# Scan operands of two directions loaded by one transfer to 128 partitions

## The chip, the cores and the metric

The kernel runs on one core of a Trainium2 chip. The metric is device microseconds of one execution. Five engines work side by side on queues of their own: TensorE (PE for matmuls, PEld for its weight loads), VectorE (DVE), ScalarE (ACT), GpSimd (POOL) and SyncE (SP). Nearly all transfers between DRAM and the on-chip memory of 128 partitions are issued by SP, in the order in which they stand in its queue, and are carried by 16 DMA engines.

## The reference

One layer of a bidirectional encoder on 2048 tokens of width 1024. Three head groups read the same normalised input: neighbourhood attention (6 heads), an mLSTM (4 heads) and a gated delta rule (6 heads). The last two are recurrences over 32 chunks of 64 tokens, once forwards and once backwards; their outputs are added. An output projection, a cross-attention and a feed-forward layer follow.

```python
def step(state, xs):                       # delta rule, one chunk of 64 tokens
    u_c, w_c, a_c, qd_c, ks_c, gl_c = xs
    v_new = u_c - jnp.einsum('bhld,bhde->bhle', w_c, state)
    o = jnp.einsum('bhld,bhde->bhle', qd_c, state) + jnp.einsum('bhls,bhse->bhle', a_c, v_new)
    state = state * jnp.exp(gl_c)[..., None, None] + jnp.einsum('bhld,bhle->bhde', ks_c, v_new)
    return state, o
...
h_fwd = mlstm_direction(qh, kh, vh, ig[0], fg[0])
h_bwd = jnp.flip(mlstm_direction(jnp.flip(qh, 2), ...), 2)
hs = head_rms((h_fwd + h_bwd).transpose(0, 2, 1, 3)).reshape(b, s, ML_WIDTH)
```

In the mLSTM every product is weighted by exponentials of running gate sums, with a running maximum as stabiliser.

## The kernel before

All is in 32 bits. Each product of a weight with an activation is made of three matmuls of rounded parts (`mm3`, L108). The program has three passes and a tail.

- **Pass A** projects the input for the delta rule and the mLSTM and prepares the scans. `gates` makes the gate quantities of a block of 512 tokens and stores the cumulated gates as rows, `g_row` (L405). `gram` does so for a pair of chunks (t of 0 to 15): it loads `kq` and the gate rows `gr` (L420), makes the Gram matrices, and stores for each direction d a tile `sc` of three operands, [token, operand, head, 64], in one store to `sc_d` (L473). The third operand, the keys times decay, is what the scan loads as `kb`. `inv` inverts the triangular matrices into `w_d`. `ml_in` projects q, k, v of the mLSTM and stores q and k to `mlc_d`, laid out [column tile of 128, partition, 2048 tokens] (L547).
- **Pass B** is the two scans, 16 steps of a pair of chunks each. Step m works on pair m forwards and pair 15 - m backwards at once: the forward chunk's rows stand on partitions 0 to 63 and its state's rows on 64 to 127, the backward ones mirrored. `gdn_scan` (delta rule) and `ml_scan` (mLSTM) each have a `load(m)` that fetches the operands of a step while the step before runs, into tiles of one or two buffers: `kb`, `ge`, `qe`, `me`, `mge`, `mqe` and `mkq` have one, so the next load into them waits until they have been read. Since the two directions need different pairs, and different halves of the partitions, each operand is loaded by two transfers of 64 partitions. Between the steps stand projections for the attention (`rest`), so that PE has work while the scans wait.
- **Pass C** is the neighbourhood attention. Its values are loaded by `nav` (L926) from `nav_d`, where rows are tokens of a 32 x 64 grid: a transfer takes up to 4 grid rows of 24 or 32 columns and 384 elements of each, and lays the tokens one on each partition.
- **The tail** is output projection, cross-attention and feed-forward layer.

A scheduler orders each engine's instructions when the program is built. The program then waits on semaphores alone.

Names in the rows below: `ge` is the gates broadcast over 64 partitions for the delta rule (768 elements each), `me` and `mge` are the stabilisers and gate factors of the mLSTM, broadcast likewise (512 elements), `kb` is the keys above, `mkq` and `mqe` are q and k of the mLSTM in two layouts. `gr` in pass A is the same gate rows, for `gram`.

Three of the loads, of the delta rule and the mLSTM, read so:

```python
nc.sync.dma_start(out=kb[CH[d]], in_=self.sc_d[d, t, :, :, 2].rearrange("c s h l -> s c h l"))
nc.sync.dma_start(out=ge[SR[d]], in_=self.g_row[t, :, d][None].broadcast_to([64, 2, 6, 64]))
nc.sync.dma_start(out=kq[:, d], in_=self.mlc_d[:, :, P * t:P * t + P].rearrange("c p l -> p c l"))
```

Of the kernel before, what the change touches and what calls it, by code (L numbers as in the profile page):

```python
# [8 lines left out]
F32 = mybir.dt.float32  # L9
# [4 lines left out]
PSUM = bass.MemoryType.PSUM  # L14
DRAM = bass.MemoryType.DRAM

P = 128
# [32 lines left out]
class Trunk:  # L50
# [26 lines left out]
    def rsqrt(self, out, in_, n):  # L77
        """out = in_ ** -0.5 on GpSimd, [P, n]."""
        self.nc.gpsimd.tensor_tensor(out=out, in0=in_, in1=self.nhalf[:in_.shape[0]].broadcast_to([in_.shape[0], n]), op=ALU.pow)

    def rms_stats(self, sq_sum, n, pspool, small, rs=None, name="psm"):
        """sq_sum [P, n] (partial sums over D per partition) -> PSUM [P, n] with 1/rms of each column on every partition.
        rs: where 1/rms stays, tokens on partitions."""
# [18 lines left out]
    def mm3(self, out, sh, sl, mh, ml, nk):  # L102
        """out += stationary.T @ moving over nk k-tiles, exact to fp32: hi*hi + hi*lo + lo*hi."""
# [8 lines left out]
    def mix(self, late):  # L112
        """x -> y_d, the three head groups' outputs, transposed; late keeps what the last blocks of attention need."""
# [6 lines left out]
        self.mlc_d = dt("mlc_d", [4, P, T])  # L120
# [4 lines left out]
        self.sc_d = dt("sc_d", [2, 16, 2, 64, 3, 6, 64])  # L125
# [27 lines left out]
    def pass_a(self, rest):  # L153
        """Projections of the delta rule and the mLSTM; Gram matrices and inverses of the delta rule."""
        with ExitStack() as st:
# [16 lines left out]
            for b in range(4):  # L172
# [16 lines left out]
                # of the last group first what the first steps of the scan need  # L189
# [7 lines left out]
    def step(self, gen, n, late=0):  # L197
        """n steps of a generator; late: how far behind their place in the program they may run."""
# [4 lines left out]
    def pass_b(self, rest):  # L203
        """The scans, with keys and values of the neighbourhood attention between their steps."""
# [15 lines left out]
    def pass_c(self, late):  # L220
        """Neighbourhood attention, with the last projections and the other heads' outputs between its blocks."""
# [17 lines left out]
    def norm_in(self, b, first=True):  # L239
        """Block b of the input, normalised: self.acts[b % 2]; the first time also the norms."""  # L240
# [3 lines left out]
        # nothing else runs before block 0: its two halves go side by side, in small pieces  # L244
# [37 lines left out]
    def gdn_in(self, b, ct):  # L282
        """q, k, v of the delta rule for one block of tokens, tile ct: projection, convolution, 2 silu, to DRAM.
        The convolution runs two tokens behind the projection."""
# [40 lines left out]
    def zero_w(self):  # L325
        """The blocks of w_d that stay zero."""
# [1073 lines left out]
```

## Time and profile before

| | |
|---|---|
| median of 3 runs | 3787.74 us (3775.37 to 3800.31) |
| span of the profiled execution | 3789.0 us (its record has no other time of its own) |
| PE busy | 3468.7 us, 92% |
| DVE, POOL, ACT busy | 1819.1, 1601.0, 1153.2 us |
| DMA | 466.07 MB in 396663 packets, mean 123 GB/s |
| steps of the scans | first matmul L672 at 856.4 us, last at 1280.2 us |

The page cuts the span into 40 slices of some 95 us. The tenth to the fourteenth hold the scans. A busy share of the DMA engines is a mean over all 16: 0.25 can be four engines that work all the time and twelve that do nothing.

### The profile page before, as it was taken

The numbers are of one execution on the slowest core, as the hardware profiler recorded it, in microseconds if no ns is written. First come the engines' busy times: TensorE is split into PE (matmuls) and PEld (weight loads), VectorE is DVE, ScalarE is ACT, GpSimd is POOL, SyncE is SP. The second block draws the span as 40 slices with busy tenths as digits, with TensorE's granted clock in tenths as the row PEclk, the third lists the DMA queues.
The fourth block names the chain that finished last, engine by engine and source line by source line (L and its number), as shares of the span: only waits on it lengthen the run. The fifth ranks groups of instructions, "written<-read, shape, count | busy, mean of one in ns | idle before, by whom it ended". The sixth has DMA issues, their size and how long they took to land.

```text
span 3789.0 us, 54073 instructions
## 1 busy us (share of the span) xinstructions
PE 3468.7 (92%) x21392; PEld 2774.0 (73%) x21392; DVE 1819.1 (48%) x3257; ACT 1153.2 (30%) x2015; POOL 1601.0 (42%) x947
## 2 busy tenths in 40 slices
PE   5878688888788889999999999999999999999998
PEld 4656566666666655588888887888888778888887
DVE  7697977625666644553443436222222352222224
ACT  3233232232323333544343344222222332222223
POOL 4455444554454531253535445333333453333333
PEclk9988888988899996999999999999999999999999
DMA  4546475678999565742233233111111141111112
GB/s 140 179 132 183 140 193 142 174 181 200 202 215 217 173 216 172 210 174 98 95 134 134 87 123 133 53 45 48 45 50 48 60 138 48 49 53 48 53 47 89
DMA packets 396663, 466.07 MB, mean 123 GB/s; under 512 B 151978, under 2 KB 296826, under 8 KB 393338
## 3 DMA queue, kind: packets, MB, share of 16 engines
q1 hardware_dynamic: 392794, 450.55, 41.2%
q0 software_dynamic: 3616, 12.06, 0.9%
q8 instruction: 169, 2.77, 0.3%
q14 instruction: 84, 0.69, 0.1%
HBM read 360.01 MB, written 102.50 MB: 122 GB/s over the span
## 4 chain that ended last, share of the span: by engine, by line
PE 52%; DVE 1%; ACT 1%; issue 1%; DMA 0%; POOL 0%; POOLq 0%; DVEq 0%; SPq 0%; ACTq 0%
PE psg L108 31%; PE psa L108 21%; PE psa L1180 0%; DVE nh L1005 0%; DVE ss L1016 0%; PE psm L88 0%; PE psm L99 0%; ACT whi L987 0%; DMA out_y<-nh 0%; DMA xb<-x_d 0%; POOL wlo L989 0%; DVE xb L1251 0%; ACT acta L1137 0%; ACT acta L1006 0%; ACT sqt L1015 0%
## 5 line engine op out<-in xcount | busy, mean ns | idle before, releaser
L989 POOL TENSOR_TENSOR wlo<-wraw,whi 128x1024 fp32r<-128x1024 f32 (+2 forms) x401 | 842.0, 2101 | 1294.1 <-ACT whi L987 1271.7
L108 PE MATMUL psg<-acta,whi 128*128 128x512 f32 x3008 | 975.3, 404 | 36.9 <-ACT pad L295 23.2
L108 PE MATMUL psg<-actb,whi 128*128 128x512 f32 (+2 forms) x2752 | 857.4, 393 | 36.8 <-DVE rt L613 10.2
L987 ACT CAST whi<-wraw 128x1024 fp32r<-128x1024 f32 (+2 forms) x417 | 373.5, 896 | 1192.3 <-PE psa L108 551.7
L108 PEld LDWEIGHTS psg<-acta,whi 128*128 128x128 f32 x3008 | 576.7, 194 | 169.2 <-ACT pad L295 25.2
L108 PE MATMUL psa<-ht,whi 128*128 128x512 f32 x2048 | 638.6, 395 | 0.6 <-ACT whi L987 0.5
L108 PEld LDWEIGHTS psg<-actb,whi 128*128 128x128 f32 (+1 forms) x2752 | 518.9, 193 | 148.2 <-ACT pad L295 11.2
L108 PE MATMUL psg<-acta,wlo 128*128 128x512 f32 x1504 | 602.5, 402 | 3.6 <-POOL wlo L989 3.6
L108 PE MATMUL psg<-actb,wlo 128*128 128x512 f32 (+2 forms) x1376 | 539.9, 393 | 27.9 <-POOL wlo L989 27.9
L108 PEld LDWEIGHTS psa<-ht,whi 128*128 128x128 f32 x2048 | 384.0, 188 | 95.1 <-ACT whi L987 1.5
L1229 DVE TENSOR_TENSOR fr<-fr 128x512 f32<-128x512 f32 x128 | 167.9, 1312 | 495.4 <-ACT fr L1228 495.4
L1242 DVE TENSOR_TENSOR xb<-psa,xb 128x512 f32<-128x512 f32 x256 | 175.6, 691 | 476.4 <-PE psa L108 476.3
L108 PE MATMUL psa<-ht,wlo 128*128 128x512 f32 x1024 | 401.0, 396 | 0.7 <-POOL wlo L989 0.7
L108 PEld LDWEIGHTS psg<-acta,wlo 128*128 128x128 f32 x1504 | 290.8, 193 | 67.6 <-POOL wlo L989 5.0
L108 PEld LDWEIGHTS psg<-actb,wlo 128*128 128x128 f32 (+1 forms) x1376 | 265.2, 193 | 86.5 <-POOL wlo L989 33.4
L1232 POOL TENSOR_TENSOR ht<-fr,ht 128x512 fp32r<-128x512 f32 x128 | 169.1, 1321 | 249.1 <-ACT ht L1231 247.8
L108 PEld LDWEIGHTS psa<-ht,wlo 128*128 128x128 f32 x1024 | 192.3, 188 | 47.5 <-POOL wlo L989 1.8
L1016 DVE TENSOR_TENSOR ss<-ss,sqt 128x512 f32<-128x512 f32 (+1 forms) x91 | 123.4, 1356 | 47.0 <-ACT sqt L1015 44.3
L308 DVE SCALAR_TENSOR_TENSOR acc<-pad,vecs,acc 128x512 f32<-128x512 f32 (+2 forms) x144 | 143.6, 1000 | 1.5 <-DVE sm L436 0.6
L1231 ACT CAST ht<-fr 128x512 fp32r<-128x512 f32 x128 | 79.4, 621 | 180.1 <-DVE fr L1229 180.0
L1228 ACT ACTIVATE fr<-psg 128x512 f32<-128x512 f32 x128 | 75.9, 593 | 132.3 <-PE psg L108 132.3
L495 DVE TENSOR_TENSOR tv<-x 72x30 f32<-72x30 f32 (+36 forms) x210 | 94.4, 470 | 2.0 <-DVE x L496 0.6
(376 smaller groups left out, 3982.3 us busy)
## 6 DMA issues: line engine op xcount, KB each, us to landing
wraw<-in_w_ff SPq DMA_DIRECT2D x72, 512.0 KB
wraw<-in_w_ff SPq DMA_DIRECT2D x144, 256.0 KB
wraw<-in_w_gd SPq DMA_DIRECT2D x36, 512.0 KB
sc_d<-sc SPq DMA_DIRECT2D x32, 576.0 KB
xt<-in_xT SPq DMA_DIRECT2D x16, 1024.0 KB
wraw<-in_w_out SPq DMA_DIRECT2D x32, 512.0 KB
wraw<-in_w_xq SPq DMA_DIRECT2D x32, 512.0 KB
wraw<-in_w_xo SPq DMA_DIRECT2D x32, 512.0 KB
```

Source lines behind the costliest of these rows:

```text
L108: nc.tensor.matmul(out=out, lhsT=a(k), rhs=b(k), start=(i == 0), stop=(i == n - 1))
L308: V.scalar_tensor_tensor(out=acc[:, :n], in0=pad[:, p0 + j:p0 + j + n], scalar=cw(j), in1=acc[:, :n], op0=ALU.mult, op1=ALU.add)
L495: V.tensor_tensor(out=tv, in0=m[:, j + 1:32, j:j + 1].broadcast_to([2 * N, n, j]), in1=m[:, j:j + 1, 0:j].broadcast_to([2 * N, n, j]), op= ...
L987: nc.scalar.copy(out=hi, in_=raw)
L989: (lo_eng or nc.gpsimd).tensor_tensor(out=lo, in0=raw, in1=hi.bitcast(F32), op=ALU.subtract)
L1016: nc.vector.tensor_tensor(out=ss, in0=ss, in1=sq, op=ALU.add)
L1228: S.activation(out=r, in_=ps, func=AF.Relu)
L1229: V.tensor_tensor(out=r, in0=r, in1=r, op=ALU.mult)
L1231: S.copy(out=ht[:, 0], in_=r)
L1232: G.tensor_tensor(out=ht[:, 1], in0=r, in1=ht[:, 0].bitcast(F32), op=ALU.subtract)
L1242: V.tensor_tensor(out=xs[nb][:, j], in0=ps, in1=xs[nb][:, j], op=ALU.add)
```

## The change

Three of the delta rule's and mLSTM's operands for both directions get a layout in DRAM in which pair m of the forward direction and pair 15 - m of the backward one are two rows at a fixed distance, so that one transfer can name both, and one transfer fills all 128 partitions: `kb` from a new array `kb_d`, `ge` from a new array `g_st` (in addition to `g_row`, which `gram` still reads), `me` from `mx_row` and `mge` from `ai_row`, which change their order of dimensions or of directions. The source of such a transfer is written as two rows, then 64 (tokens for `kb`, a repetition for the other three), then 768 or 512 elements. In pass A the store of `sc` becomes three: operands 0 and 1, and the halves of `kb`. `g_st` takes 16 small stores for each block of 512 tokens. `mlc_d` is laid out by pair, [pair, partition, column tile, 128], so `mkq` reads 2 KB runs in place of 512 bytes, the store of q and k writes 512-byte runs in place of 2 KB, and `mqe` takes two transfers per direction in place of one. `mx_row` and `ai_row` are stored by two transfers each. Nothing that is computed changes.

```diff
-        self.mlc_d = dt("mlc_d", [4, P, T])
+        self.mlc_d = dt("mlc_d", [16, P, 4, P])
...
-        self.sc_d = dt("sc_d", [2, 16, 2, 64, 3, 6, 64])
+        self.sc_d = dt("sc_d", [2, 16, 2, 64, 2, 6, 64])
+        self.kb_d = dt("kb_d", [2, 16, 64, 2, 6, 64])
+        self.g_st = dt("g_st", [2, 16, 2, 6, 64])
...
         for c in range(2):
             nc.sync.dma_start(out=self.g_row[t4, c].rearrange("t d h l -> t (d h) l"), in_=row[:, 64 * c:64 * c + 64])
 
+            for t in range(4):
+                for d in range(2):
+                    nc.sync.dma_start(out=self.g_st[1 - d, 4 * b + t, c], in_=row[12 * t + 6 * d:12 * t + 6 * d + 6, 64 * c:64 * c + 64])
...
-            nc.sync.dma_start(out=self.sc_d[d, t].rearrange("c s a h l -> (c s) (a h l)"), in_=sc.rearrange("p a h l -> p (a h l)"))
+            nc.sync.dma_start(out=self.sc_d[d, t].rearrange("c s a h l -> (c s) (a h l)"), in_=sc[:, 0:2].rearrange("p a h l -> p (a h l)"))
+            for c2 in range(2):
+                nc.sync.dma_start(out=self.kb_d[d, t, :, c2], in_=sc[64 * c2:64 * c2 + 64, 2])
...
-                nc.sync.dma_start(out=self.mlc_d[ct, :, sl], in_=t)
+                nc.sync.dma_start(out=self.mlc_d[sl.start // P:sl.stop // P, :, ct].rearrange("j p l -> p j l"), in_=t.rearrange("p (j l) -> p j l", l=P))
...
+            nc.sync.dma_start(out=kb.rearrange("p c h l -> p (c h l)"), in_=self.kb_d.rearrange("d t s c h l -> (d t) s (c h l)")[m:32 - m:31 - 2 * m])
             for d in range(2):
...
-                nc.sync.dma_start(out=kb[CH[d]], in_=self.sc_d[d, t, :, :, 2].rearrange("c s h l -> s c h l"))
...
-                nc.sync.dma_start(out=ge[SR[d]], in_=self.g_row[t, :, d][None].broadcast_to([64, 2, 6, 64]))
+            nc.sync.dma_start(out=ge.rearrange("p c h l -> p (c h l)"), in_=self.g_st.rearrange("d t c h l -> (d t) (c h l)")[15 - m:17 + m:2 * m + 1, None].broadcast_to([2, 64, 768]))
...
-                nc.sync.dma_start(out=kq[:, d], in_=self.mlc_d[:, :, P * t:P * t + P].rearrange("c p l -> p c l"))
-                nc.sync.dma_start(out=e[CH[d]], in_=self.mx_row[None, :, d, t].broadcast_to([64, 2, 4, 64]))
+                nc.sync.dma_start(out=kq[:, d], in_=self.mlc_d[t])
...
-                nc.sync.dma_start(out=qe[SR[d]], in_=self.mlc_d[0:2, :, P * t:P * t + P].rearrange("c (h e) l -> e (c h) l", h=2))
-                nc.sync.dma_start(out=ge[SR[d]], in_=self.ai_row[d, t].rearrange("h c l -> (h c l)")[None].broadcast_to([64, 512]).rearrange("p (h l) -> p h l", l=P))
+                for a in range(2):
+                    nc.sync.dma_start(out=qe[SR[d], a::2], in_=self.mlc_d[t, CH[a], 0:2])
+            nc.sync.dma_start(out=e.rearrange("p c h l -> p (c h l)"), in_=self.mx_row.rearrange("d t c h l -> (d t) (c h l)")[m:32 - m:31 - 2 * m, None].broadcast_to([2, 64, 512]))
+            nc.sync.dma_start(out=ge.rearrange("p h l -> p (h l)"), in_=self.ai_row.rearrange("d t h c l -> (d t) (h c l)")[15 - m:17 + m:2 * m + 1, None].broadcast_to([2, 64, 512]))
```

The scheduler orders the changed program anew. In a middle step of the scans SP's queue held these loads before (the last numbers are the destination's partitions and elements):

```order
L637 DMA kb<-sc_d 64x2x384
L640 DMA qe<-gd_c 64x6x128
L641 DMA ge<-g_row 64x2x384
L637 DMA kb<-sc_d 64x2x384
L640 DMA qe<-gd_c 64x6x128
L641 DMA ge<-g_row 64x2x384
L833 DMA mkq<-mlc_d 128x4x128
L836 DMA mqe<-mlc_d 64x4x128
L834 DMA me<-mx_row 64x2x256
L837 DMA mge<-ai_row 64x512
```

In a middle step of the changed program SP's queue holds these:

```order
L641 DMA kb<-kb_d 128x1x768
L847 DMA mqe<-mlc_d 64x2x128
L844 DMA mkq<-mlc_d 128x512 x2
L847 DMA mqe<-mlc_d 64x2x128
L848 DMA me<-mx_row 128x1x512
L648 DMA qe<-gd_c 64x6x128 x2
L649 DMA ge<-g_st 128x1x768
L849 DMA mge<-ai_row 128x1x512
```

The joined loads stand one behind the other in the queue, each once per step, and their destinations are written as 128 x 1 x N, which is how the program spells a transfer whose source has one dimension more, here two rows of 64.

The same spelling stands in pass C of the program before, at the loads of the values, whose sources are 4 (or 3) grid rows of 32 tokens; SP's queue there:

```order
L926 DMA nav<-nav_d 72x1x384
L929 DMA naqb<-nac_d 128x3x128
L920 DMA nab<-in_nab 128x2x352
L926 DMA nav<-nav_d 128x1x384 x2
L926 DMA nav<-nav_d 96x1x384
L929 DMA naqb<-nac_d 128x3x128
```

These loads are the same in both programs; nothing moves here.

In pass A, behind the first block's gates, SP's queue held before:

```order
L417 DMA kq<-gd_c 128x9x128 x2
L405 DMA g_row<-row 4x12x64 x2
L547 DMA mlc_d<-rt 128x512
L420 DMA gr<-g_row 64x768 x4
L985 DMA wraw<-in_w_ml 128x1024
```

SP's queue at the same place in the changed program:

```order
L423 DMA kq<-gd_c 128x9x128 x2
L407 DMA g_row<-row 4x12x64
L411 DMA g_st<-row 6x64 x4
L426 DMA gr<-g_row 64x768
L411 DMA g_st<-row 6x64 x4
L407 DMA g_row<-row 4x12x64
L411 DMA g_st<-row 6x64 x2
L426 DMA gr<-g_row 64x768
L411 DMA g_st<-row 6x64 x6
L426 DMA gr<-g_row 64x768 x2
```

The 16 small stores stand before and among the loads of `gr`, on which the first `gram` of the block depends.

## Rows read from the trace of the kernel before

**Rows 1.** The page: span, engines, 40 slices, and the chain by engine.
```profile
span 3789.0 us, 54073 instructions
...
PE 3468.7 (92%) x21392; PEld 2774.0 (73%) x21392; DVE 1819.1 (48%) x3257; ACT 1153.2 (30%) x2015; POOL 1601.0 (42%) x947
...
PE   5878688888788889999999999999999999999998
...
DMA  4546475678999565742233233111111141111112
...
PE 52%; DVE 1%; ACT 1%; issue 1%; DMA 0%; POOL 0%; POOLq 0%; DVEq 0%; SPq 0%; ACTq 0%
```

**Rows 2.** Five stretches: each engine's busy us, granted clock, DMA share, GB/s.
```profile
core 0: us, PE busy (x) PEld busy (x) DVE busy (x) ACT busy (x) POOL busy (x), PEclk, DMA share, GB/s
812.00:1285.00 473.00, 385.22 (x5493) 315.67 (x5491) 278.63 (x533) 139.06 (x266) 232.64 (x158) 0.91 0.87 203
...
1080.00:1200.00 120.00, 103.09 (x1514) 84.17 (x1509) 77.18 (x149) 37.70 (x73) 59.16 (x43) 0.97 0.96 227
1509.00:1511.00 2.00, 2.00 (x15) 1.67 (x15) 1.41 (x5) 1.56 (x5) 0.00 (x0) 0.50 0.25 86
1513.00:1516.00 3.00, 3.00 (x17) 1.69 (x18) 1.95 (x8) 1.23 (x5) 0.00 (x0) 1.00 1.02 309
```

**Rows 3.** The scans' tiles: count, ns min/median/max, first and last start.
```profile
L642 ACT ACTIVATE ge<-ge x16: 842/844/847, 828.1 to 1227.7; 128x768 f32<-128x768 f32 x16
...
L672 PE MATMUL pss<-sc,wp x768: 219/222/369, 856.4 to 1280.2; 128*64 128x64 f32 x192
```

**Rows 4.** Waits from 812 to 1285 us: us in total, times, longest.
```profile
ACT ge L642 <- DMA ge<-g_row: 77.4, 13, 11.0
...
DVE me L838 <- DMA me<-mx_row: 44.4, 14, 6.6
```

**Rows 5.** DMA from 812 to 1285 us: totals, then issues, KB each.
```profile
DMA packets 84514, 95.81 MB, mean 203 GB/s; under 512 B 8742, under 2 KB 69526, under 8 KB 84294
...
mkq<-mlc_d SPq DMA_DIRECT2D x32, 256.0 KB
...
kb<-sc_d SPq DMA_DIRECT2D x32, 192.0 KB
...
ge<-g_row SPq DMA_DIRECT2D x32, 192.0 KB
...
me<-mx_row SPq DMA_DIRECT2D x32, 128.0 KB
...
mge<-ai_row SPq DMA_DIRECT2D x32, 128.0 KB
```

**Rows 6.** SP's issues from 1505 to 1511 us: start, us, line, tiles, count.
```profile
1505.90 1.16 SPq L926 DMA_DIRECT2D nav<-nav_d  x2
1507.16 0.43 SPq L977 DMA_DIRECT2D y_d<-nat  x1
1507.64 1.55 SPq L926 DMA_DIRECT2D nav<-nav_d  x2
1509.29 1.16 SPq L920 DMA_DIRECT2D nab<-in_nab  x1
```

**Rows 7.** DMA from 1504 to 1524 us, in 40 slices of half a us.
```profile
DMA  0000002176222279999999994899894222213799
GB/s 0 0 0 0 0 0 25 37 244 223 83 86 89 86 144 240 272 368 271 283 339 314 327 319 122 202 301 308 280 342 181 88 89 70 79 73 131 207 297 373
```

**Rows 8.** Pass A: SP's issues of two stretches, and a wait (100 to 700 us).
```profile
463.50 1.37 SPq L405 DMA_DIRECT2D g_row<-row  x2
...
326.24 0.94 SPq L473 DMA_DIRECT2D sc_d<-sc  x2
...
DVE gr L439 <- DMA gr<-g_row: 33.8, 11, 11.5
```

More of the change, by code (lines that the diff above doesn't have):

```diff
@@ L636, in load @@
                 nc.sync.dma_start(out=wp[CH[d], d].rearrange("p c h l -> p (c h) l"), in_=self.w_d[d][g][:, 12 * (t - GROUPS[g][0]):12 * (t - GROUPS[g][0]) + 12])
-                nc.sync.dma_start(out=kb[CH[d]], in_=self.sc_d[d, t, :, :, 2].rearrange("c s h l -> s c h l"))
-                nc.sync.dma_start(out=sc[CH[d], d, :, 0:2].rearrange("p c a h l -> p c (a h l)"), in_=self.sc_d[d, t, :, :, 0:2].rearrange("c s a h l -> s c (a h l)"))
+                nc.sync.dma_start(out=sc[CH[d], d, :, 0:2].rearrange("p c a h l -> p c (a h l)"), in_=self.sc_d[d, t].rearrange("c s a h l -> s c (a h l)"))
                 nc.sync.dma_start(out=sc[CH[d], d, :, 2].rearrange("p c h l -> p c (h l)"), in_=self.v_d[t].rearrange("c s h l -> s c (h l)"))
                 nc.sync.dma_start(out=qe[SR[d]], in_=self.gd_c[0:3, :, P * t:P * t + P].rearrange("c (h e) l -> e (c h) l", h=2))
-                nc.sync.dma_start(out=ge[SR[d]], in_=self.g_row[t, :, d][None].broadcast_to([64, 2, 6, 64]))
+            nc.sync.dma_start(out=ge.rearrange("p c h l -> p (c h l)"), in_=self.g_st.rearrange("d t c h l -> (d t) (c h l)")[15 - m:17 + m:2 * m + 1, None].broadcast_to([2, 64, 768]))
             nc.scalar.activation(out=ge, in_=ge, func=AF.Exp)
@@ L731, in ml_prep @@
         V = nc.vector
-        self.mx_row = dr.tile([2, 2, 16, 4, 64], F32, name="mx_row")
+        self.mx_row = dr.tile([2, 16, 2, 4, 64], F32, name="mx_row")
         self.ai_row = dr.tile([2, 16, 4, 2, 64], F32, name="ai_row")
@@ L786, in ml_prep @@
         V.tensor_tensor(out=mx, in0=pm, in1=mr[:, :, 0:1].broadcast_to([P, 2, 64]), op=ALU.max)
-        nc.sync.dma_start(out=self.mx_row.rearrange("c d t h l -> (d t h) c l"), in_=mx)
+        for ch in range(2):
+            nc.sync.dma_start(out=self.mx_row[:, :, ch].rearrange("d t h l -> (d t) h l"), in_=mx[:, ch])
         V.tensor_tensor(out=t0, in0=mr[:, :, 0:1].broadcast_to([P, 2, 64]), in1=mx, op=ALU.subtract)
         nc.scalar.activation(out=t0, in_=t0, func=AF.Exp)
-        nc.sync.dma_start(out=self.ai_row.rearrange("d t h c l -> (d t h) (c l)"), in_=flat3(t0))
+        for d in range(2):
+            nc.sync.dma_start(out=self.ai_row[1 - d].rearrange("t h c l -> (t h) (c l)"), in_=flat3(t0)[R[d]])
         V.tensor_tensor(out=t0, in0=rb, in1=mx, op=ALU.add)
```

## The prediction

> **What bounds the kernel now.** I began with the page: PE is busy for 92% of the span, and the chain that ended last is almost all PE [rows 1]. A change in transfers can only matter where PE is not full, so I went along the slices: PE stands at 5 to 8 tenths in the first fifteen, and in the scans the DMA line goes to 9 [rows 1]. The table of stretches says it closely: from 812 to 1285 us the 16 DMA engines are busy for 0.87 of the time and move 203 GB/s, and from 1080 to 1200 us for 0.96, while PE works 385 of 473 us [rows 2]. The scans are near the limit of the DMA engines, and the waits there agree: ACT waits 77.4 us in all for `ge` and DVE 44.4 us for `me` [rows 4], two of the loads that are changed. A step takes (1227.7 - 828.1) / 15 = 26.6 us, by the exponential on `ge`, one per step [rows 3]. So the question is what the change does to the time that a DMA engine needs per step; with the engines at 0.87 there is no cover for more work on them.
>
> **How many engines carry a joined load.** The trace of before has no load that is joined like the new ones, but it has one that is written the same way: `nav`, whose source is 4 or 3 grid rows of 32 tokens and whose destination is 128 or 96 partitions. At 1505.90 to 1509.19 us SP issues four of them, one small store, and then a bias load `nab` at 1509.29 [rows 6]. Before `nab` begins to move, the DMA engines are busy for a share of 0.25, with 86 GB/s, from 1509 to 1511 us [rows 2], and the fine slices show twos there in a row, at 83 to 89 GB/s, before and again after 1519 us [rows 7]. A share of 0.25 is four engines of 16, though more loads were queued than one: the next one waits behind the first on the same four, and twelve idle. As soon as `nab` moves, whose two sides both begin with 128 partitions, all are busy: 1.02 and 309 GB/s [rows 2] (packets overlap a little). So I read the trace as follows: a transfer is divided over engines by the outermost count of both sides, four for `nav`, and always over the same ones. The joined `kb`, `ge`, `me` and `mge` begin with two rows. Two engines then carry each of them, and the same two all four. (The step from four to two is an inference; no transfer of before begins with two.)
>
> The Trainium skill ("DMA: Bandwidth & Descriptors", section "Why a DMA increments its semaphore by 16 and not by 1") states such a rule: the number is the largest up to 16 that divides the slowest dimension other than 1 on both sides. By that rule `nav` has four engines and the joined loads two; the trace's 0.25 agrees with the first, and no run yet shows the second.
>
> **The change part by part.** All from the profiled execution, whose span of 3789.0 us is 1.3 us above the median; the runs reach 0.35% to either side, so a difference of 1% is about what can be told from none.
>
> *The joined loads.* They stand in the stretch of 473 us, with 32 issues of 192 KB each for `kb` and `ge` and 32 of 128 KB for `me` and `mge` [rows 5]: 32 x 640 KB x 1024 = 20.97 MB, the same bytes before and after. Before, each of 16 engines carries 1.31 MB of it; now each of two carries 10.49 MB. A lone engine's rate is 86 / 4 = 21.5 GB/s [rows 2], at best 373 / 16 = 23.3 in the fastest half microsecond with all engines [rows 7]; in the crowded scans it is 203 / (16 x 0.87) = 14.6 [rows 2]. The two engines work mostly alone, as those of `nav` did, so I take 21.5: 488 us, at best 450. That alone is as long as the whole stretch is today, or 30.5 us per step against 26.6.
>
> *All else on these two engines.* The stretch moves 95.81 MB [rows 5]; less 20.97, a sixteenth is 4.68 MB per engine. At 14.6 GB/s it takes 321 us, at 21.5 218 us, at 23.3 201 us. I take 218, since the other 14 engines are mostly done when these two get to it. Every other load of a step also has a share on the two engines and is complete only when that share is, so nothing gets around them.
>
> *Sum for the scans.* 488 + 218 = 706 us of work for each of the two engines. They will not be without gaps: the tiles have one buffer, and SP waits in order for each to be read. The fullest stretch of before had 0.96 [rows 2]; 706 / 0.96 = 735 us, which is 262 us more than 473 (46 per step). The fast end is 450 + 201 = 651 without gaps, +178; the slow end 488 + 321 = 809 at 0.96, or 843, +370. The fast end has one more reserve: the loads of the first two steps can be issued early, beside pass A's end, as those of the first step are today (`ge` is ready at 828.1, the scan's matmul starts at 856.4 [rows 3]); two steps of 30.5 us off +178 are +117. PE has 88 us of idle time in the stretch now and would have some 350; that it is slower at the lower clock then granted (0.91 there now [rows 2]) stays inside the idle time.
>
> *mkq in 2 KB runs.* 32 loads of 256 KB are 8.39 MB, 0.52 MB for each of 16 engines: 36 us at 14.6, 24 us at 21.5. This is within the 321 or 218 us above, so it has no term of its own. `mqe`, twice as many transfers of half the size, moves the same runs of 512 bytes: nothing on the engines; on SP it costs two issues more per step, where the joined loads save four.
>
> *The stores of pass A.* 16 small stores per block, at 1.37 / 2 = 0.69 us for an issue of the like [rows 8], are 11 us in which the loads of `gr` stand back; DVE already waits 33.8 us for those in pass A [rows 8]. For four blocks at most 44 us, and at least nothing, where DVE is busy with something else. The 64 more stores of `kb` cost 0.47 us of SP each [rows 8], 30 us in all, spread over the pass; who waits for SP's queue there are the next weights and the next `kq`, both fetched ahead, so nothing to 30 us. Of the two together I take 10 us, near the lower end: the whole wait for `gr` is now 3 us in each of 11 cases [rows 8], and DVE has other work there.
>
> Total: 3789 + 262 + 10 = 4061 us.
>
> **The rivals.**
>
> *The joined loads use all 16 engines* (the change does what it looks like). Then they gain: loads of 64 partitions run at 14.6 GB/s per engine in the scans, loads of 128 at 309 / 16 = 19.3 [rows 2]. 1.31 MB per engine fall from 90 to 68 us, at best to the half, 45; with `mkq` (12 us) that is 34 to 57 us off a stretch that is at 0.87 to 0.96. With the 10 us of pass A: 3789 - 45 + 10 = 3754 us, from 3732 to 3765. This is the case on the other side: not slower. What decides is the share of DMA in a joined load. For it: the waits for `ge` and `me` [rows 4]. Against it: the 0.25 of `nav`, written the same way [rows 2, 7]. The Trainium skill ("SBUF — State Buffer", section "Door 1: The DMA port swizzle") says that 64 partitions reach half of the memory's ports and 128 all; by that rule the joined loads are faster, which needs them to be spread over the engines first. The trace's 14.6 against 19.3 is at least in its direction.
>
> *Two engines, but other ones each time.* Then the load is even over 16 and only the latency of one load grows: 64 rows on one engine, 192 KB / 21.5 GB/s = 9.1 us for `kb`. The time stays within some 30 us, 3790. Against it: with several `nav` loads queued the share stays at 0.25 and doesn't double [rows 6, 7].
>
> *Pass A is held up more than I take*, SP being the bound there: 44 + 30 = 74 us in place of 10, on top of any of these; with the first, 4125 us.
>
> **How the numbers follow.** Two engines, the same ones: 0.84, 4061 us, from 3789 + 117 = 3906 to 3789 + 370 + 74 = 4233. All 16 engines: 0.11, 3754 us; by its bounds half of it lies more than 1% below. Changing pairs: 0.05, no change. The range is the likeliest case's own, 3900 to 4230, and leaves out less than 2 in 10. Faster by over 1%: 0.06; within 1%: 0.10; slower: 0.84.
>
> **What would show it.** In the profile after: a stretch of the scans of some 735 us in place of 473, with 46 us from one exponential on `ge` to the next; a DMA share that falls to about a half, with long runs of ones (2 of 16 engines, 0.12) at some 43 GB/s; waits of ACT for `ge`, of DVE for `me` and of PE for `kb` that grow by some 15 us per step; nothing changed behind the scans. Wrong would be a share of 0.9 in the scans with a shorter step (all engines), or a step as long as before with a low share (something else than the engines' work bounded the scans). If the step lies between 36 and 41 us, the lone engine is faster than I took; if pass A ends more than 30 us later, its stores cost more.

## The result, and the profile after

The changed kernel takes 4129.89 us (median of 4 runs, 4121.6 to 4149.26) against 3781.55 us (4 runs, 3773.07 to 3800.31): a ratio of 1.0919, with a 95% interval of 1.0886 to 1.0952. The profiled execution grew from a span of 3789.0 us to 4119.8 us, by 330.8. Of the page after, these are the span, the engines, three lines of the 40 slices and the chain:

```profile
span 4119.8 us, 54195 instructions
...
PE 3509.9 (85%) x21392; PEld 2805.2 (68%) x21392; DVE 1794.2 (44%) x3257; ACT 1153.4 (28%) x2015; POOL 1583.3 (38%) x947
...
PE   5878788865445556988999999999999999999998
...
PEclk9888888877767778988999999999999999999999
...
DMA  4638567554444445567423333321111132111112
...
PE 48%; issue 1%; DVE 1%; ACT 1%; DMA 0%; POOL 0%; SPq 0%; POOLq 0%; DVEq 0%; ACTq 0%
```

Beside [rows 1], one place differs: the slices of the scans, where PE falls from 8 to 4 and 5 tenths and DMA, which stood at 8 and 9, to 4. Both are less busy there than before, so neither PE nor the DMA engines as a whole hold the scans up. To see how much of the 330.8 us lies where, I cut both executions at the first load of the scans, at the first matmul of the recurrence (the first `pss<-sc,wp`, L672 before, L680 after) and at the last one. The table of these stretches before (columns as in [rows 2]):

```profile
0.00:811.90 811.90, 643.20 (x4278) 505.82 (x4279) 629.24 (x1277) 246.92 (x349) 402.20 (x215) 0.87 0.58 160
811.90:856.40 44.50, 36.63 (x320) 29.19 (x318) 6.11 (x11) 11.09 (x18) 18.59 (x11) 0.92 0.97 212
856.40:1280.20 423.80, 344.25 (x5139) 283.03 (x5140) 270.11 (x516) 127.12 (x246) 211.59 (x147) 0.90 0.87 203
1280.20:3789.00 2508.80, 2444.61 (x11667) 1955.96 (x11663) 913.63 (x1453) 768.06 (x1402) 968.66 (x576) 0.98 0.29 96
```

and after:

```profile
0.00:843.50 843.50, 658.76 (x4258) 517.50 (x4259) 621.94 (x1277) 246.05 (x348) 390.45 (x215) 0.85 0.59 154
843.50:928.20 84.70, 47.87 (x361) 37.93 (x360) 5.42 (x10) 13.14 (x22) 17.02 (x10) 0.74 0.48 118
928.20:1595.80 667.60, 357.21 (x5112) 291.85 (x5110) 248.84 (x516) 119.26 (x237) 193.85 (x144) 0.74 0.45 124
1595.80:4119.80 2524.00, 2446.03 (x11672) 1957.87 (x11667) 917.97 (x1455) 774.91 (x1408) 982.01 (x579) 0.98 0.30 96
```

Pass A is 31.6 us longer, the lead from the first load to the first step 40.2 us, the scans 243.8 us, all behind them 15.2 us. In the scans nearly the same matmuls (5112 and 5139) keep PE busy for 13 us more (its granted clock is 0.74 there, 0.90 before), and the other 231 us are idle time of PE (667.6 - 357.2 = 310.4 us against 79.6). Who waits there is seen in the scans' tiles after, with the count, ns min/median/max and the first and last start,

```profile
L650 ACT ACTIVATE ge<-ge x16: 842/842/843, 877.2 to 1531.3; 128x768 f32<-128x768 f32 x16
...
L680 PE MATMUL pss<-sc,wp x768: 221/222/370, 928.2 to 1595.8; 128*64 128x64 f32 x192
```

and in the waits after from 843 to 1600 us (us in total, times, longest):

```profile
ACT ge L650 <- DMA ge<-g_st: 241.4, 16, 22.6
...
DVE me L850 <- DMA me<-mx_row: 199.9, 15, 22.6
...
POOL msc L871 <- DMA mge<-ai_row: 67.0, 5, 35.1
```

A step takes (1531.3 - 877.2) / 15 = 43.6 us, 17 us more than in [rows 3]. The wait for `ge` is 15.1 us in each step and that for `me` 13.3, against 77.4 and 44.4 us in all [rows 4]. The same bytes come in joined issues now: of the DMA view of the stretch from 843 to 1601 us the totals and two of the loads (KB each):

```profile
DMA packets 63816, 92.66 MB, mean 122 GB/s; under 512 B 7278, under 2 KB 39390, under 8 KB 63758
...
kb<-kb_d SPq DMA_DIRECT2D x16, 384.0 KB
...
ge<-g_st SPq DMA_DIRECT2D x16, 384.0 KB
```

And this is what the DMA engines do while these loads run. 40 slices of half a microsecond, from 1140 to 1160 us:

```profile
DMA  1111111197111479998798893311196999999998
GB/s 49 45 47 49 49 49 49 57 324 225 49 49 49 98 221 258 271 193 177 174 127 188 344 340 111 82 47 41 47 168 209 374 187 187 202 261 259 200 172 166
```

The table of stretches for the first 3.5 us of it:

```profile
1140.00:1143.50 3.50, 0.00 (x0) 0.00 (x0) 0.00 (x0) 1.75 (x3) 0.00 (x0) 0.50 0.13 48
```

The ones are what the twos were in [rows 7]: a share of 0.13 of 16 engines is two engines, with 48 GB/s, 24 GB/s each, and PE does nothing at all in those 3.5 us.

Each packet of the trace has a start and a duration, so one can count how many are in flight at a time (packets of one engine overlap a little, so the count is near the number of busy engines, not equal to it). Over the stretch from 843 to 1601 us there is none for 44 us, one for 12, exactly two for 308 (at 46 GB/s), exactly four for 16, and more than twelve for 234. A pair that changed from one joined load to the next would show fours; there are hardly any.

SP's queue slows as well. SP issues the loads in order, and a load that isn't joined, `qe`, takes longer to issue after (first line) than in run 1 below (second line), where nothing is joined:

```profile
L648 SPq DMA_DIRECT2D qe<-gd_c x32: 574/1166/6698, 847.1 to 1513.9; - x32
...
L650 SPq DMA_DIRECT2D qe<-gd_c x32: 573/600/1247, 857.2 to 1246.8; - x32
```

All its 315 issues between the first and the last matmul of the recurrence take 405 us, the 376 of run 1 take 220.

### The profile page after: what moved, and what is told of

Its sections match the earlier page's. It is cut to its first block, busy times and chain, and to the rows that moved or that the text cites. A ratio compares the mean times of both kernels' runs of the same rounds, so it can differ in the third digit from the quotient of the medians.

```text
span 4119.8 us, 54195 instructions
## 1 busy us (share of the span) xinstructions
PE 3509.9 (85%) x21392; PEld 2805.2 (68%) x21392; DVE 1794.2 (44%) x3257; ACT 1153.4 (28%) x2015; POOL 1583.3 (38%) x947
## 4 chain that ended last, share of the span: by engine, by line
PE 48%; issue 1%; DVE 1%; ACT 1%; DMA 0%; POOL 0%; SPq 0%; POOLq 0%; DVEq 0%; ACTq 0%
PE psg L108 28%; PE psa L108 19%; PE psa L1192 0%; DMA wraw<-in_w_ff 0%; DVE nh L1017 0%; PE psm L99 0%; ACT whi L999 0%; DVE ss L1028 0%; PE psm L88 0%; DMA out_y<-nh 0%; POOL wlo L1001 0%; DVE xb L1263 0%; ACT acta L1149 0%; ACT acta L1018 0%; DVE nh L1263 0%
## 5 line engine op out<-in xcount | busy, mean ns | idle before, releaser
L108 PEld LDWEIGHTS psg<-acta,whi 128*128 128x128 f32 x3008 | 579.9, 195 | 179.2 <-ACT pad L297 25.2
L108 PE MATMUL psg<-actb,wlo 128*128 128x512 f32 (+2 forms) x1376 | 542.2, 395 | 19.3 <-POOL wlo L1001 19.3
L108 PEld LDWEIGHTS psg<-acta,wlo 128*128 128x128 f32 x1504 | 292.6, 195 | 77.8 <-POOL wlo L1001 12.6
L108 PEld LDWEIGHTS psg<-actb,wlo 128*128 128x128 f32 (+1 forms) x1376 | 266.6, 194 | 77.4 <-POOL wlo L1001 23.6
L1028 DVE TENSOR_TENSOR ss<-ss,sqt 128x512 f32<-128x512 f32 (+1 forms) x91 | 120.3, 1322 | 51.5 <-ACT sqt L1027 48.4
L850 DVE TENSOR_TENSOR me<-cmx,me 128x512 f32<-128x512 f32 x16 | 11.1, 692 | 282.0 <-DMA me<-mx_row 199.9
L680 PE MATMUL pss<-sc,wp 128*64 128x64 f32 x768 | 40.6, 251 | 98.7 <-ACT sc L690 69.7
```

What stands on the lines that cost most here:

```text
L108: nc.tensor.matmul(out=out, lhsT=a(k), rhs=b(k), start=(i == 0), stop=(i == n - 1))
L680: nc.tensor.matmul(out=ps[CH[d], 64 * h:64 * h + 64], lhsT=wp[:, d, cc[d], h], rhs=sc[:, d, cc[d], 2, h], start=True, stop=True)
L850: V.tensor_tensor(out=e, in0=self.cmx[:, :, m, :, None].broadcast_to([P, 2, 4, 64]), in1=e, op=ALU.subtract)
L1028: nc.vector.tensor_tensor(out=ss, in0=ss, in1=sq, op=ALU.add)
```

## The experiments

The theory that stood behind the prediction, A: two of the 16 engines carry every joined load, the same two, and their work sets the step. Its rival D: the engines' work is no limit; what costs is only that the reader of a joined load waits longer for it. Beside them stood the question which of the new stores hold up pass A. In the table each run is cut as above: until the first matmul of the recurrence, the scans from its first to its last, and all behind them, by the profiled execution, us. Ratios are to the kernel before on the same chip, with 95% intervals. Runs 1 to 4, 5 to 8, and 9 and 10 each have a chip of their own, on which the median of before is 3791.40, 3784.34 and 3786.24 us; so a difference of two totals from different chips is uncertain by some 10 us.

| kernel | until the scans | scans | behind | median | ratio |
|---|---|---|---|---|---|
| before | 856.4 | 423.8 | 2508.8 | 3781.55 | 1 |
| after | 928.2 | 667.6 | 2524.0 | 4129.89 | 1.0919 (1.0886 to 1.0952) |
| 1 split | 901.3 | 395.7 | 2518.0 | 3820.73 | 1.0083 (1.0060 to 1.0107) |
| 2 spread | 896.0 | 397.5 | 2538.9 | 3836.01 | 1.0119 (1.0099 to 1.0140) |
| 3 `kb` joined | 911.3 | 489.4 | 2528.4 | 3928.32 | 1.0365 (1.0340 to 1.0390) |
| 4 `ge` joined | 909.8 | 488.1 | 2564.8 | 3962.01 | 1.0443 (1.0416 to 1.0469) |
| 5 copy on two | 1001.1 | 391.1 | 2522.1 | 3903.91 | 1.0336 (1.0311 to 1.0361) |
| 6 copy on sixteen | 892.5 | 400.7 | 2534.8 | 3829.73 | 1.0136 (1.0108 to 1.0163) |
| 7 no `g_st` | 899.9 | 402.7 | 2512.1 | 3819.68 | 1.0117 (1.0091 to 1.0143) |
| 8 no `g_st`, no `kb_d` | 856.7 | 385.8 | 2539.2 | 3781.11 | 1.0002 (0.9985 to 1.0019) |
| 9 copy in the scans, two | 891.2 | 461.9 | 2542.3 | 3895.73 | 1.0286 (1.0233 to 1.0339) |
| 10 copy in the scans, sixteen | 895.8 | 402.6 | 2521.0 | 3820.82 | 1.0088 (1.0054 to 1.0121) |

**1. The split kernel.** The changed kernel with all its layouts, but each of the four joined loads written as two of 64 partitions:

```diff
-nc.sync.dma_start(out=kb.rearrange("p c h l -> p (c h l)"), in_=self.kb_d.rearrange("d t s c h l -> (d t) s (c h l)")[m:32 - m:31 - 2 * m])
+for d in range(2):
+    t = m if d == 0 else 15 - m
+    nc.sync.dma_start(out=kb[CH[d]].rearrange("p c h l -> p (c h l)"), in_=self.kb_d[d, t].rearrange("s c h l -> s (c h l)"))
...
+for d in range(2):
+    t = m if d == 0 else 15 - m
+    nc.sync.dma_start(out=ge[SR[d]].rearrange("p c h l -> p (c h l)"), in_=self.g_st[1 - d, t].rearrange("c h l -> (c h l)")[None].broadcast_to([64, 768]))
```

`me` and `mge` are split in the same way.

> The changed kernel with its new layouts and stores, but each of the four joined loads (kb, ge, me, mge) is made by two transfers of 64 partitions again, one per direction. Theory A (the two engines that carry a joined load are what costs): the scans fall back to about 473 us with a DMA share near 0.87, and what is left over the kernel before is pass A's stores and the new layout of q and k: 3785 to 3820 us, ratio 1.00 to 1.01. Theory B (a large part of the 348 us comes from the 128 more stores in pass A, from 512-byte runs in the store of q and k, or from the doubled mqe): the time stays above 3900 us, ratio over 1.03.

3820.73 us: of the 348 us that the change costs, 309 are gone. The stretch of the scans of the split kernel:

```profile
901.30:1297.00 395.70, 328.59 (x5130) 268.64 (x5130) 255.95 (x501) 121.65 (x240) 198.31 (x146) 0.90 0.84 210
```

The share of the DMA engines is back at 0.84, and the clock at 0.90. So the joining is the cause of these 309 us, not the layouts. The scans are even 28 us shorter than before, while their start stays 45 us later.

**2. The same two loads joined, but over sixteen engines.** `kb_d` is ordered by step, so that a source has 128 rows, and `g_st` holds each row eight times (its stores in pass A write it so), so that it has 16; `kb` and `ge` are joined loads to 128 partitions, `me` and `mge` are split.

```diff
-self.kb_d = dt("kb_d", [2, 16, 64, 2, 6, 64])
-self.g_st = dt("g_st", [2, 16, 2, 6, 64])
+self.kb_d = dt("kb_d", [16, 2, 64, 2, 6, 64])
+self.g_st = dt("g_st", [16, 16, 2, 6, 64])
...
+nc.sync.dma_start(out=kb.rearrange("p c h l -> p (c h l)"), in_=self.kb_d[m].rearrange("d s c h l -> (d s) (c h l)"))
+nc.sync.dma_start(out=ge.rearrange("p c h l -> p (c h l)"), in_=self.g_st[m].rearrange("r c h l -> r (c h l)")[:, None].broadcast_to([16, 8, 768]))
```

> As the kernel with four split loads, but kb and ge are joined to 128 partitions from layouts whose source begins with 128 and with 16 rows: kb_d is ordered by step of the scan, and g_st holds each row 8 times, so that a load of ge reads 16 rows 8 times each. Theory A (the number of engines decides): all 16 engines carry both loads, nothing like the 348 us is seen, the time is that of the split kernel or somewhat less, since 12.6 MB move at the rate of 128 partitions (19.3 against 14.6 GB/s per engine, 14 us less, at best 27): 3755 to 3810 us. Theory C (a transfer to 128 partitions is dear by itself, or a wait for both directions at once costs): it is slower than the split kernel by 50 us or more.

It is a join to 128 partitions all the same, and the loss is gone: scans of 397.5 us. Its exponentials on `ge`, one per step:

```profile
L651 ACT ACTIVATE ge<-ge x16: 842/842/846, 862.0 to 1240.3; 128x768 f32<-128x768 f32 x16
```

That is 25.2 us per step; the split kernel has (1254.8 - 869.2) / 15 = 25.7. The gain that a full-width load was meant to bring is half a microsecond per step by this exponential, and nothing by the length of the scans (397.5 against 395.7). The whole is 15 us slower than the split kernel, by what stands behind the scans, and outside the 3755 to 3810 us that I had expected.

**3 and 4. One joined load alone.** The split kernel with `kb` alone, or `ge` alone, as the changed kernel loads it. Against the split kernel, run 3 and, below the dots, run 4:

```diff
-for d in range(2):
-    t = m if d == 0 else 15 - m
-    nc.sync.dma_start(out=kb[CH[d]].rearrange("p c h l -> p (c h l)"), in_=self.kb_d[d, t].rearrange("s c h l -> s (c h l)"))
+nc.sync.dma_start(out=kb.rearrange("p c h l -> p (c h l)"), in_=self.kb_d.rearrange("d t s c h l -> (d t) s (c h l)")[m:32 - m:31 - 2 * m])
...
-for d in range(2):
-    t = m if d == 0 else 15 - m
-    nc.sync.dma_start(out=ge[SR[d]].rearrange("p c h l -> p (c h l)"), in_=self.g_st[1 - d, t].rearrange("c h l -> (c h l)")[None].broadcast_to([64, 768]))
+nc.sync.dma_start(out=ge.rearrange("p c h l -> p (c h l)"), in_=self.g_st.rearrange("d t c h l -> (d t) (c h l)")[15 - m:17 + m:2 * m + 1, None].broadcast_to([2, 64, 768]))
```

> As the kernel with four split loads, but kb alone is joined with a source of two rows, as in the changed kernel. Theory A in its form of work (two engines have more to carry than a step lasts): kb puts 8 us per step on two engines (197 kB at 24.5 GB/s), and with the rest, 14 to 23 us, the sum is 22 to 31 us per step, near the 26.6 us that a step lasts: 0 to 70 us over the split kernel. Theory D (each joined load costs by its own longer way, some 8 us more to land, on the path of a step): 16 times 8, about 130 us over the split kernel; the four together would then be more than the 348 us seen, unless they overlap.

> As the kernel with four split loads, but ge alone is joined with a source of two rows. Theory A in its form of work: ge has the same bytes as kb, so the same 0 to 70 us over the split kernel, within 20 us of the kernel with kb joined. Theory D (the way of each load): ge is the load that ACT waits for most, 241 us after the change, so it costs about 130 us or more, and clearly more than kb.

Each costs much: 108 us for `kb`, 141 for `ge`. I had looked for 0 to 70 and was wrong; by the totals alone theory D, which asked for 130 and for more of `ge`, is nearer. In the scans, though, the two, of the same bytes, cost the same, 93.7 and 92.4 us over the split kernel's 395.7; the difference between the totals stands behind the scans. And the reader of `kb` doesn't wait: in run 3 PE waits 6.3 us for it, once. Who waits is ACT, for `ge`, which is a split load there; the first two lines are waits of run 3 from 850 to 1420 us, the third is one of the split kernel from 850 to 1350.

```profile
ACT ge L652 <- DMA ge<-g_st: 176.2, 16, 16.8
...
PE pss L663 <- DMA kb<-kb_d: 6.3, 1, 6.3
...
ACT ge L654 <- DMA ge<-g_st: 87.8, 16, 10.7
```

So one joined load makes the readers of other loads wait. The tile rows of the recurrence in the two kernels, `kb` joined first:

```profile
L682 PE MATMUL pss<-sc,wp x768: 216/222/369, 911.3 to 1400.7; 128*64 128x64 f32 x192
```

```profile
L682 PE MATMUL pss<-sc,wp x768: 221/222/368, 909.8 to 1397.9; 128*64 128x64 f32 x192
```

One load puts 16 x 0.393 MB x (1/2 - 1/16) = 2.75 MB more on each of the two engines, 115 us at 24 GB/s, and 93 us of it come out as time. All four put 9.18 MB more on them, 382 us, and 272 us come out (667.6 - 395.7). Where the rest goes isn't shown, since the trace doesn't name the engine of a packet. At most one packet is in flight for 0.13 of the scans in the split kernel and for 0.13 with `kb` joined, so it isn't stretches in which all engines stood still. Gaps of the two engines alone, or a faster rate of theirs when the others fall idle, remain.

**5 and 6. A copy that nobody reads.** In every step of the split kernel a copy of `kb`'s two rows within DRAM, with two rows outermost (run 5), or as two copies of 64 rows (run 6).

```diff
+nc.sync.dma_start(out=self.dc_d[m, :, :, 0:768], in_=self.kb_d.rearrange("d t s c h l -> (d t) s (c h l)")[m:32 - m:31 - 2 * m])
...
+for d in range(2):
+    t = m if d == 0 else 15 - m
+    nc.sync.dma_start(out=self.dc_d[m, d, :, 0:768], in_=self.kb_d[d, t].rearrange("s c h l -> s (c h l)"))
```

> The kernel with four split loads, and in each step one transfer more that nobody waits for: the two rows of kb's source (2 x 64 x 768 elements, 393 kB) are copied from DRAM to a DRAM array that is read nowhere, in the same form as the joined kb, so that two engines carry it. Theory A (two engines have more to carry, and every other load has its share on them): at 24.5 GB/s it puts 8 us per step on the two engines, and since the step of the split kernel (25.7 us) is itself near what the engines need, the step grows by 6 to 9 us and the time by 100 to 150 us: 3915 to 3970 us. Theory D (a joined load costs because its own reader waits longer for it): no reader, so no cost beyond that of the same bytes on 16 engines: 3820 to 3860 us.

> The same copy that nobody waits for, as two transfers of 64 rows, which 16 engines carry. Theories A and D agree: 393 kB are 24.6 kB per engine, 1 to 1.7 us per step, 15 to 30 us in all over the split kernel: 3835 to 3855 us. If it costs as much as the copy on two engines, the bytes and not the number of engines are the cause.

By the totals this speaks for A: on the same chip and for the same bytes, the copy on two engines costs 74 us more than that on sixteen (over the split kernel, on another chip, 83 and 9 us by the medians, 96 and 20 by the ratios). But the place isn't the one that both texts speak of. SP's issues of the copy in run 5:

```profile
L652 SPq DMA_DIRECT2D dc_d<-kb_d x16: 528/661/8660, 520.7 to 821.8; - x16
```

Nothing depends on the copies, so the scheduler put all of them ahead of the scans, into pass A, and it is pass A that got longer (the recurrence starts at 1001.1 in place of 901.3 us). The scans themselves take 391.1 us, no more than without. The runs show that two busy engines hold up others' transfers in pass A, and not yet that they do so in the scans. Hence the next two.

**9 and 10. The copy inside the scans.** The copy now reads the step output of three steps before, so it can't be issued before that step has run: 13 copies of 0.393 MB.

```diff
+if m >= 3:
+    nc.sync.dma_start(out=self.dc_d[m, :, 0:128, 0:384], in_=self.ho_d[m - 3, :, :, 256:640].rearrange("p a n -> a p n"))
...
+if m >= 3:
+    for d in range(2):
+        nc.sync.dma_start(out=self.dc_d[m, d, 0:128, 0:384], in_=self.ho_d[m - 3, :, d, 256:640])
```

> The split kernel with one more transfer in each of 13 steps of the delta rule's scan, read by nobody: a copy in DRAM of the step output of three steps before (two rows of 128 x 384 floats, 0.39 MB, as much as the two halves of kb), with two rows outermost, so on two engines. It waits for that output, so it can't be moved ahead of the scans as the copy of the fifth run was. The computation is whole. Theory A (the engines' work): 13 x 0.197 MB per engine at 24.5 GB/s is 104 us of two engines, and the split step has almost none to spare (kb alone cost 6.7 us a step, ge alone 7.2): scan from first to last matmul 60 to 105 us longer than the split kernel's 395.7, total 3880 to 3930. Theory D (only the wait of the one who reads the slow transfer): nobody reads it, scan within 15 us of the split kernel's, total 3815 to 3835.

> The same copy of the step output in the same place, as two transfers of 128 rows each, so on sixteen engines. The computation is whole. Theory A: 13 x 0.025 MB per engine, some 13 us of the engines in all: scan 5 to 20 us longer than the split kernel's, total 3825 to 3845. Theory D: as the copy on two engines, within 15 us of the split kernel. If the bytes or the places in SP's queue are what costs, this run is as slow as the copy on two engines.

The issues of the copy and the recurrence of run 9,

```profile
L653 SPq DMA_DIRECT2D dc_d<-ho_d x13: 594/607/657, 923.9 to 1305.3; - x13
...
L687 PE MATMUL pss<-sc,wp x768: 219/222/369, 891.2 to 1353.1; 128*64 128x64 f32 x192
```

and the recurrence of run 10:

```profile
L688 PE MATMUL pss<-sc,wp x768: 219/222/369, 895.8 to 1298.4; 128*64 128x64 f32 x192
```

The copies are issued all along the scans. On two engines they make the scans 66 us longer than the split kernel's, on sixteen 7 us, with two issues in place of one; the totals of the two, on the same chip, are 75 us apart. No engine reads the copy, so D as it stands falls. The waits of run 9 from 850 to 1380 us (first line) and of run 10 (second) say who waits: DVE for `me`, which is a split load there. ACT's wait for `ge` has not grown (68.7 us against 82.0).

```profile
DVE me L861 <- DMA me<-mx_row: 142.0, 14, 44.1
...
DVE me L862 <- DMA me<-mx_row: 77.5, 15, 42.8
```

But SP's queue does wait for the copy. Of its waits in run 9 over the same time seven lines name the copy, 48.7 us in all and 13 times, as many as there are copies; these are the longest. In run 10 none does.

```profile
SPq L648 <- DMA dc_d<-ho_d: 12.8, 3, 4.5
...
SPq L1008 <- DMA dc_d<-ho_d: 8.2, 2, 4.3
...
SPq L649 <- DMA dc_d<-ho_d: 7.3, 2, 4.0
```

So the loads behind a slow transfer can be late in two ways: their own shares queue on the two engines, or SP issues them later. Both go back to the slow transfer on the two engines; no run here separates them, nor shows why SP waits there. The copy of run 9 puts 13 x 0.393 / 2 = 2.56 MB on each of the two engines, 106 us at 24 GB/s, and 66 come out as time, less than of `kb` joined with nearly the same work (93). Why less isn't shown; it isn't that PE waits for `kb`, which is 6.3 us.

**7 and 8. The stores of pass A.** Two suspects for its later end: the stores of `g_st` (A1) and the three-way store of `sc` (A2). Run 7 is the split kernel without the stores of `g_st` (`ge` is loaded from `g_row`); run 8 is run 7 with `sc` in one store again, and `kb` loaded from `sc_d`. What is left of the change in run 8 are `mlc_d` by token tile, the two transfers of `mqe`, and the order of `mx_row` and `ai_row`.

```diff
-for t in range(4):
-    for d in range(2):
-        nc.sync.dma_start(out=self.g_st[1 - d, 4 * b + t, c], in_=row[12 * t + 6 * d:12 * t + 6 * d + 6, 64 * c:64 * c + 64])
...
+    nc.sync.dma_start(out=ge[SR[d]], in_=self.g_row[t, :, d][None].broadcast_to([64, 2, 6, 64]))
...
-nc.sync.dma_start(out=self.sc_d[d, t].rearrange("c s a h l -> (c s) (a h l)"), in_=sc[:, 0:2].rearrange("p a h l -> p (a h l)"))
-for c2 in range(2):
-    nc.sync.dma_start(out=self.kb_d[d, t, :, c2], in_=sc[64 * c2:64 * c2 + 64, 2])
+nc.sync.dma_start(out=self.sc_d[d, t].rearrange("c s a h l -> (c s) (a h l)"), in_=sc.rearrange("p a h l -> p (a h l)"))
...
+    nc.sync.dma_start(out=kb[CH[d]], in_=self.sc_d[d, t, :, :, 2].rearrange("c s h l -> s c h l"))
```

> The kernel with four split loads, without the 64 small stores of g_st in pass A; ge is loaded from g_row as in the kernel before. The split kernel is 30 us slower than before, although its scans are 28 us shorter: its first scan matmul comes 45 us later. Theory A1 (the small stores stand before the loads of gr): 20 to 40 us of the 45 come back, 3780 to 3800 us. Theory A2 (the 64 more stores of kb, 64 partitions each, hold SP and the engines): little comes back, 3810 to 3820 us.

> Without the stores of g_st and without kb_d: the third operand stays in sc_d and kb is loaded from it as before. What is left of the change is q and k of the mLSTM by token tile and the order of mx_row and ai_row, all loads of 64 partitions or by token tile. By both theories pass A ends as in the kernel before; if the shorter scans come from mkq's longer runs they stay, and the time is 3755 to 3785 us, below before; if they come from kb's longer runs, it is 3785 to 3800 us.

Without the 64 stores of `g_st` nothing changes that shows: 3819.68 against 3820.73 us, on two chips, with ratios of 1.0117 and 1.0083 whose intervals overlap. Without the three-way store of `sc`, on the same chip as run 7, 39 us are gone, and the recurrence starts at 856.7 us, as before. The table of run 8, cut like those above:

```profile
0.00:814.50 814.50, 650.69 (x4281) 511.72 (x4282) 625.95 (x1277) 247.34 (x349) 406.40 (x215) 0.87 0.59 160
814.50:856.70 42.20, 35.92 (x317) 28.65 (x315) 5.41 (x10) 9.44 (x16) 15.02 (x9) 0.91 0.94 217
856.70:1242.50 385.80, 322.41 (x5091) 262.56 (x5090) 260.45 (x509) 121.68 (x241) 201.26 (x145) 0.91 0.87 216
1242.50:3781.70 2539.20, 2461.64 (x11715) 1971.22 (x11710) 914.49 (x1462) 775.12 (x1409) 981.19 (x579) 0.97 0.30 96
```

The scans are 38.0 us shorter than before, and yet the total is the same (1.0002), since what stands behind them is 30.4 us longer and the span is 7.3 us shorter. PE is busy for 22 us less in the shorter scans, with 48 matmuls fewer, and for 2461.6 us behind them against 2444.6, with 52 more: a part of the filling work that ran between the steps has moved behind them, where PE has no room. The granted clock there is also 0.97 against 0.98; how much of the 30.4 us each makes up wasn't separated. Of all versions none is faster than the kernel before.

## Why the prediction was right

The forecast was 4061 us, 272 us above the profiled execution of before; the profiled executions are 331 apart, the medians 348. Of the 59 us that the forecast lacks against the 331, 22 lie in pass A, 22 in the stretch of the scans and 15 behind them. The mechanism of the likeliest case held; a sign of it, a wait, and some sizes did not.

*Two engines, the same two for all joined loads.* Inferred from `nav` [rows 2, 7]; now shown by the ones at 0.13 and 48 GB/s. That this is what costs is shown by the loss going with the split, and by the join over sixteen engines that loses nothing. The Trainium skill's rule ("DMA: Bandwidth & Descriptors", section "Why a DMA increments its semaphore by 16 and not by 1") gives two for these loads, and this trace agrees, with its 0.13 of 16. That they are always the same two follows from the count of packets, two for 308 us and four for 16, with four such loads in each step. The prediction's reading of `nav` was a little too smooth: after 1519 us its twos stand at 70 to 89 GB/s, not at 83 to 89 [rows 7].

*Sum for the scans.* 735 us were foreseen for the stretch from the first load on; it is 84.7 + 667.6 = 752 us to the last matmul of the recurrence. Both terms held. The work of each of the two engines is 10.49 MB plus (92.66 - 20.97) / 16 = 4.48 MB, 14.97 MB. In the 758 us from 843 to 1601 at least two packets are in flight for 702 us, so the two can be busy for at most 0.93 of the stretch, where 0.96 was taken; and 14.97 MB in 702 us are 21.3 GB/s, where 21.5 was taken. They have hardly any time off: the mean rate per packet in flight, summed over the 702 us, makes some 14 of the 14.97 MB. That 21.5 fitted is in part luck. It was taken because the two would work mostly alone. They are alone for 308 of the 758 us, at 46 GB/s, 23 each, and at 24 in the slices above; while more than twelve packets are in flight, for 234 us, the rate per packet is 16 GB/s. The forecast lies between the two.

The step is 43.6 us; I had 46. The waits for `ge` and `me` grew by some 10 us per step each, to 15.1 and 13.3 us, where 15 were foreseen. The third wait named as a sign did not grow: PE was to wait some 15 us longer for `kb` in each step, and waits 4.8 us in all, once, of the waits after from 812 to 1601 us:

```profile
PE pss L661 <- DMA kb<-kb_d: 4.8, 1, 4.8
```

The work on the two engines comes out at other loads than the one that made it, as in run 3.

*The fill of the first steps* I named as a reserve (loads issued early). It was a cost: the lead to the first matmul of the recurrence grew by 40.2 us, with the DMA share at 0.48 in place of 0.97. In the split kernel it is 48.4 us, from the first load at 852.9 us, so 36 of the 40 go with the joining.

*mkq in 2 KB runs* had no term. Run 8 has scans 38 us shorter with the new layouts of the mLSTM alone, so they may be worth something there; a part of the 38 is PE's filling work that moved behind the scans (22 us of PE's time). That it comes to nothing in the total goes at least in part with that, and not with what I argued, that it is part of the engines' other work. Which of the three edits left in run 8 shortens the scans wasn't separated.

*The stores of pass A* were taken at 10 us, within 0 to 74. Pass A ended 31.6 us later, and by runs 7 and 8 the pair costs some 40. I put the weight on the wrong one: the 64 stores of `g_st` take 294 ns each in the trace after and not 0.69 us, and the wait for `gr` has not grown (32.9 us against the 33.8 of [rows 8]):

```profile
L411 SPq DMA_DIRECT2D g_st<-row x64: 257/294/977, 137.5 to 669.2; - x64
...
L481 SPq DMA_DIRECT2D kb_d<-sc x64: 445/579/1096, 153.1 to 731.5; - x64
...
  DMA gr<-g_row: 32.9, 8
```

The stores of `kb_d` take 64 x 0.579 = 37 us of SP's time, near the 30 foreseen, and the run without the three-way store is 39 us shorter. By which wait isn't settled: the waits of pass A after show no new one of that size, and the scheduler orders all of pass A anew with these stores, which a run that leaves the stores out doesn't tell from the stores themselves.

*PE's slower clock* was to stay inside its idle time. It did in the scans (13 us more of busy time there, beside 231 us more of idle). In pass A it did not: PE's busy time until the first load grew by 15.6 us, half of the 31.6, at a granted clock of 0.85 against 0.87.

*Behind the scans* I foresaw nothing; it is 15.2 us, and over all the runs of the table that part lies between 2508.8 and 2564.8 us, for nearly the same work (11625 to 11715 matmuls). PE's busy time behind the scans moves with it: 2430.7 us for 11703 matmuls in the split kernel, at a granted clock of 0.98, and 2480.8 us for 11701 with `ge` joined, at 0.96. So what differs between these two is the clock, not the work. A gain of some 40 us in the scans can vanish into that spread, as in run 8.

*Rivals.* All 16 engines: refuted by the ones. Run 2, which is that case built for two of the four loads, shows that its gain isn't there either: 22 to 45 us were reckoned for the four joined loads, 13 to 27 for these two by their 12.6 of 20.97 MB, and the scans are 397.5 us long against 395.7, with 0.5 us less per step at most. The Trainium skill's advice to use one transfer of 128 partitions in place of two to disjoint halves ("DMA: Bandwidth & Descriptors", section "Rules for kernel authors") holds here only as far as the joined source still spreads: with two rows outermost it cost 309 us, with 128 and 16 rows it brought half a microsecond per step at most. Changing pairs: refuted by the step. Pass A held up more: in part true, 40 us.

## What to carry to other kernels

When two transfers are joined, look at the outermost count on both sides, and not at the partitions that are filled: a source written as two rows gives the work of sixteen engines to two, and in a crowded stage other loads wait behind it, whoever reads it. A low DMA share beside long waits for loads is the sign; divide the GB/s by the engines that the share stands for. The load whose reader waits need not be the slow one: here `kb` cost 94 us of the scans while its own reader waited 6. If a stage is shortened by taking waits out of it, see what work filled those waits, since it has to run elsewhere.

## What the runs showed that I had not expected

- A pair of engines alone moved 45 to 49 GB/s, 24 per engine, where four moved 83 to 89 from 1509 to 1511 us [rows 7], 21 to 22 per engine, and sixteen 203 in the scans at a share of 0.87 [rows 2], 14.6 per busy engine. But sixteen also moved 309 from 1513 to 1516 us [rows 2], 19.3 each. That the number of busy engines alone sets the rate isn't shown, since the transfers differ.
- A copy within DRAM that nobody reads cost 74 us more on two engines than on sixteen in pass A, and 75 us more in the scans, though it took fewer issues.
- With `kb` alone joined, PE waited 6.3 us for `kb`, and ACT 176.2 us in place of 87.8 for `ge`, which wasn't joined.
- 64 stores of 1.5 KB took 294 ns each to issue and cost no time that shows; 64 stores of 98 KB (64 x 384 floats) took 579 ns each and, with the new order, some 40 us.
- Scans 38 us shorter left the total where it was (run 8, ratio 1.0002).
